# Forming the down-projection's weight sums in the stage that uses them, in an encoder block on one core

## The chip, the cores and the metric

The kernel runs on one core of one Trainium2 chip. The time is the device time of one execution in microseconds; 3 runs of the kernel before gave a median of 3151.03 us, from 3148.64 to 3153.19 us. A core has TensorE for matmuls, VectorE, ScalarE and GpSimd for elementwise work, each with its own instruction order, and here the queue of SyncE, from which the transfers between HBM and the on-chip memory are issued, one after the other. In the rows these are PE (PEld for its weight loads), DVE, ACT, POOL and SP.

## What is computed

One layer of an encoder on 2048 tokens of 1024 numbers in float32: a norm, an input projection, two groups of heads (a gated linear recurrence in both directions, and a latent attention), an output projection with residual, a second norm, a gated feed-forward part with residual, and a last norm. The change lies in the feed-forward part, whose inner width is 2816:

```python
h = _rmsnorm(x, norm2_g[l])
x = x + (jax.nn.silu(h @ w_gate[l]) * (h @ w_up[l])) @ w_down[l]
return _rmsnorm(x, final_norm_g)
```

## The kernel before

Every product is taken three times: an operand is split into a high part, rounded by ScalarE (names ending in h), and a **remainder** (ending in l), the operand less the high part, formed by VectorE or GpSimd. `mm3` (lines 193 to 195) multiplies high by high, high by remainder and remainder by high into the same bank. Splitting below means both steps.

The two large products of the feed-forward part are done as a scheme with seven products P1 to P7 in place of eight (Strassen's, in Winograd's form): both factors are cut into 2 x 2 blocks, and the seven products take blocks or sums of blocks. On the weight side these are B11 for P1, B21 for P2, B22 for P3, and the sums T4 for P4, T1 for P5, T2 for P6 and T3 for P7 (`B_OF`); T1 = B12 - B11, T3 = B22 - B12, T2 = B22 - T1, T4 = B21 - T2. The other side has A11, A12, A22, S1 to S4 (`A_OF`).

**Out-projection and second norm** (lines 1153 to 1192) go tile by tile over 16 token tiles. Each writes its part of the seven operands of the next stage to HBM (`h2_d`); `op_raw` reads them back in four pieces each, through a ring of three buffers, and `op_split` splits them with ScalarE (line 975) and VectorE (976).

**Gate and up** run in two halves (`hf`) of 1024 tokens, 22 rounds each, a round being one column block of 128 of the inner width. A round is seven products (`product`) of 12 matmuls. `r_load` loads its four weight pieces of 256 KB (B11, B12, B22, B21; line 993), all four at the time when the round before has its P1 prepared; `t_make` forms the four sums on GpSimd (line 1002), `b_make` splits, five products ahead of use (lines 1017 and 1019). `after` combines the banks on VectorE and ScalarE (lines 1079 to 1090) and stores the results g and their sums to HBM. At the end of the first half the last round's products release the operands of that half, and the seven operands of the second are loaded and split there (`late`).

**Down sums.** In the first half, `down_sums` (called 22 times, beside P2) reads four pieces of `w_down` of 128 KB (line 1061), forms the sums T1 to T4 with four operations on VectorE (1062 to 1065) and stores them in HBM (`wt_d`, line 1068). All this uses a ring of five buffers.

**Down** has 66 steps, P1, P2, P6, P7, P4, P5 with 11 steps each, of 24 matmuls into eight banks, and then P3 in eight parts of 33 matmuls. For each step `g_op` loads 512 KB of g (ring of three) and splits it on ScalarE (1253) and VectorE (1254), and `w_op` loads 256 KB of weights, a block of `w_down` or a sum from `wt_d` (ring of four, `wr`), and splits it on ScalarE (1244, names dh) and GpSimd (1245, names dl), two steps ahead. In the P5 steps `w_op` also prepares the P3 weights. When a product's last step is done, `down_after` combines its banks on VectorE, and `residual` adds x on GpSimd (line 1267): 16 times after P7, while P4 runs.

Instructions of an engine run in the order that a scheduler in the program's build has found from the program's dependences; the code above is only where they come from. A buffer of a ring is taken again when its readers are done, so a load can wait, and with it all that stands behind it on SyncE's queue.

## Time and profile before

| | before |
|---|---|
| median of 3 runs | 3151.03 us (3148.64 to 3153.19) |
| the profiled execution | 3152.19 us |
| its span, first to last instruction | 3150.4 us |
| TensorE busy | 2995.2 us, 95% of the span, 16377 matmuls |
| VectorE / ScalarE / GpSimd busy | 1915.5 (61%) / 1258.1 (40%) / 1119.5 (36%) us |
| mean granted clock of TensorE | 0.983 of full speed |
| read from HBM / written | 230.84 / 133.17 MB |

The profiled execution's own time is 1.8 us longer than its span and 1.2 us above the median. Gate and up begin at about 1780 us, the second half at about 2260, the down stage runs from about 2700 us, its P4 from 2950, its P5 from 3014, P3 from 3075. The granted clock has two levels, 1.2 and 2.4 GHz; a figure between them is a mean over the stretch. Busy time of a pipelined engine is no measure of its speed, so the number of matmuls in a stretch is read with it. A few matmul records are missing in a trace, so counts are compared with counts.

### The profile page before, as it was taken

The numbers are of one execution on the slowest core, as the hardware profiler recorded it, in microseconds if no ns is written. First come the engines' busy times: TensorE is split into PE (matmuls) and PEld (weight loads), VectorE is DVE, ScalarE is ACT, GpSimd is POOL, SyncE is SP. The second block draws the span as 40 slices with busy tenths as digits, with TensorE's granted clock in tenths as the row PEclk, the third lists the DMA queues.
The fourth block names the chain that finished last, engine by engine and source line by source line (L and its number), as shares of the span: only waits on it lengthen the run. The fifth ranks groups of instructions, "written<-read, shape, count | busy, mean of one in ns | idle before, by whom it ended". The sixth has DMA issues, their size and how long they took to land.

```text
span 3150.4 us, 45441 instructions
## 1 busy us (share of the span) xinstructions
PE 2995.2 (95%) x16377; PEld 2497.9 (79%) x16377; DVE 1915.5 (61%) x4074; ACT 1258.1 (40%) x2365; POOL 1119.5 (36%) x998
## 2 busy tenths in 40 slices
PE   7999999999789999999989888899999999999998
PEld 6899877777677888888877666788778888888786
DVE  6116557777676888888888776644654444433236
ACT  5101366666324555555533332233433333333243
POOL 1110232332332121111023554566556665234552
PEclk9999999999899999999999999999999999999999
DMA  5221112222553011100267566533433333645544
GB/s 177 72 64 55 61 60 86 80 84 80 200 189 107 28 46 34 34 24 23 94 186 226 166 210 197 187 101 101 142 119 101 104 104 97 219 154 176 183 138 153
DMA packets 335936, 366.99 MB, mean 116 GB/s; under 512 B 23480, under 2 KB 246240, under 8 KB 335712
## 3 DMA queue, kind: packets, MB, share of 16 engines
q1 hardware_dynamic: 330016, 357.00, 35.3%
q0 software_dynamic: 4608, 4.20, 0.5%
...
HBM read 230.84 MB, written 133.17 MB: 116 GB/s over the span
## 4 chain that ended last, share of the span: by engine, by line
PE 59%; DVE 8%; DMA 6%; issue 2%; POOL 1%; ACT 1%; SPq 1%; DVEq 0%; ACTq 0%; POOLq 0%
PE pd_P L195 4%; PE pd_P L194 4%; PE pd_P L193 4%; PE t L885 3%; PE pb L193 3%; PE pb L194 3%; PE pb L195 3%; PE pa L193 2%; PE pc L195 2%; PE pc L194 2%; PE pc L193 2%; PE pa L195 2%; PE pa L194 2%; PE s L852 2%; PE o L193 2%
## 5 line engine op out<-in xcount | busy, mean ns | idle before, releaser
L198 ACT ACTIVATE pth<-t 128x512 fp32r<-128x512 f32 x256 | 153.8, 603 | 249.2 <-PE t L885 249.2
L1254 DVE TENSOR_TENSOR gl_P<-gr_P,gh_P 128x1024 fp32r<-128x1024 f32 x66 | 91.1, 1381 | 218.8 <-ACT gh_P L1253 217.4
L194 PE MATMUL pd_P<-dl_P,gh_P 128*128 128x512 f32 x528 | 206.5, 391 | 3.8 <-POOL dl_P L1245 3.8
L859 DVE TENSOR_REDUCE mx<-s 128x1 f32<-128x512 f32 x256 | 175.6, 687 | 55.7 <-PE s L852 55.6
L193 PE MATMUL pd_P<-dh_P,gh_P 128*128 128x512 f32 x528 | 206.2, 391 | 0.2 <-DVE t1d L1316 0.2
L195 PE MATMUL pd_P<-dh_P,gl_P 128*128 128x512 f32 x528 | 206.1, 390 | 0.0
L868 ACT ACTIVATE pr<-s,nb 128x512 f32<-128x512 f32 x256 | 172.9, 690 | 15.2 <-DVE nb L862 11.3
L199 DVE TENSOR_TENSOR ptl<-t,pth 128x512 fp32r<-128x512 f32 x256 | 175.2, 686 | 2.5 <-ACT pth L198 0.5
L193 PE MATMUL o<-pth,vh 128*128 128x256 f32 x512 | 164.7, 322 | 0.3 <-DVE nb L862 0.3
L885 PEld LDWEIGHTS t<-ident,pr 128*128 128x128 f32 x1024 | 126.4, 140 | 40.3 <-issue 1.7
L885 PE MATMUL t<-ident,pr 128*128 128x128 f32 x1024 | 153.9, 273 | 4.1 <-DVE pr L875 2.9
L1253 ACT ACTIVATE gh_P<-gr_P 128x1024 fp32r<-128x1024 f32 x66 | 69.9, 1059 | 189.1 <-PE pd_P L194 172.0
L195 PE MATMUL o<-pth,vl 128*128 128x256 f32 x512 | 143.9, 281 | 0.0
L194 PE MATMUL o<-ptl,vh 128*128 128x256 f32 x512 | 143.9, 281 | 0.0
L651 POOL CAST qh<-qraw 128x256 fp32r<-128x256 f32 x31 | 12.4, 401 | 351.3 <-PE s L849 351.2
L875 DVE TENSOR_SCALAR pr<-pr,ri 128x512 f32<-128x512 f32 x256 | 128.3, 516 | 2.2
L194 PEld LDWEIGHTS pd_P<-dl_P,gh_P 128*128 128x128 f32 x528 | 99.4, 188 | 25.5 <-POOL dl_P L1245 4.8
L1002 POOL TENSOR_TENSOR T<-B12r,B11r 128x512 f32<-128x512 f32 x44 | 63.8, 1449 | 153.9 <-DMA B12r<-in_w_up_dram 153.9
L193 PEld LDWEIGHTS pd_P<-dh_P,gh_P 128*128 128x128 f32 x528 | 99.5, 188 | 21.6 <-DVE t1d L1316 0.6
L195 PEld LDWEIGHTS pd_P<-dh_P,gl_P 128*128 128x128 f32 x528 | 99.5, 189 | 20.7
L487 POOL TENSOR_TENSOR Am<-az 64x128 f32<-64x128 f32 x64 | 44.2, 690 | 195.3 <-DVE az L484 171.2
L1085 DVE TENSOR_TENSOR U<-t,pb 128x512 f32<-128x512 f32 x44 | 30.1, 685 | 134.0 <-PE pb L195 134.0
...
## 6 DMA issues: line engine op xcount, KB each, us to landing
s_gA<-g SPq DMA_DIRECT2D x66, 256.0 KB, 3.1
s_gS<-gS SPq DMA_DIRECT2D x66, 256.0 KB, 2.5
...
B11r<-in_w_gate_dram SPq DMA_DIRECT2D x44, 256.0 KB, 2.9
B12r<-in_w_up_dram SPq DMA_DIRECT2D x44, 256.0 KB, 2.9
B22r<-in_w_up_dram SPq DMA_DIRECT2D x44, 256.0 KB, 3.2
B21r<-in_w_gate_dram SPq DMA_DIRECT2D x44, 256.0 KB, 3.3
```

What stands on the lines that cost most here:

```text
L193: PE.matmul(ps, a_hi, b_hi, start=first, stop=False, skip_group_check=more)
L194: PE.matmul(ps, a_hi, b_lo, start=False, stop=False, skip_group_check=more)
L195: PE.matmul(ps, a_lo, b_hi, start=False, stop=last, skip_group_check=more)
L198: ACT.activation(hi, ps, AF.Copy)
L199: DVE.tensor_tensor(lo, ps, fr(hi), op=ALU.subtract)
L859: last_mx[0] = DVE.tensor_reduce(mx[:, b:b + 1], ps, op=ALU.max, axis=AX.X)
L868: ACT.activation(PR[i][:, b, :], SB[i][b], AF.Exp, scale=SCALE, bias=nb, accum_out=rs[:, b:b + 1])
L875: DVE.tensor_scalar(PR[i][:, b, :], PR[i][:, b, :], ri, None, op0=ALU.mult)
L885: PE.transpose(ps[:, j, :], PR[i][:, b, j * P:(j + 1) * P], ident)
L1002: POOL.tensor_tensor(R[nm, n], R[a, n], R[b, n], op=ALU.subtract)
L1253: ACT.activation(hi, raw, AF.Copy)
L1254: DVE.tensor_tensor(lo, raw, fr(hi), op=ALU.subtract)
```

## The change

`down_sums` and its HBM arrays go. `w_op` loads blocks of `w_down` alone and forms the sums itself on GpSimd: for P6 T3 = B22 - B12 and T2 = T3 + B11 (three loads, two operations), both kept on chip (pool `ft`); P7 takes the kept T3, without a load; P4 forms T4 = B21 - T2 from the kept T2; P5 forms T1 = B12 - B11 (two loads). The ring `wr` keeps its four buffers. The pools for the P3 weights and operands are opened only at P5's first step, after `ft` is closed.

In gate and up, `r_load` is called with names and spread over a round: B11 and B12 with P1, B22 with P6, B21 with P2; the ring has seven buffers for six, that of T four for five, that of g six for five, that of `op_raw` four for three. In the first round, A12, S1 and S3 are read through a pool of their own with five buffers, each as a group ahead of a product, and A22 and S4 are asked for earlier. At the half change an operand is split after the next product, not the one after that. The diff:

```diff
-    def op_raw(hf, i):
+    def op_raw(hf, i, pl=None, bufs=4):
...
-            raws.append(fwr.tile([P, 512], F32, tag="opraw", name=f"opr_{hf}_{i}_{j}", bufs=3))
+            raws.append((pl or fwr).tile([P, 512], F32, tag="opraw", name=f"opr_{hf}_{i}_{j}", bufs=bufs))
...
-    def r_load(n):
-
+    def r_load(n, *which):
+
+        if n >= len(seq):
+            return
         hf, f = seq[n]
         fs = slice(f * P, (f + 1) * P)
-        for nm, w_, k0 in (("B11", w_gate, 0), ("B12", w_up, 0), ("B22", w_up, 512), ("B21", w_gate, 512)):
-            raw = R[nm, n] = fwr.tile([P, 4, P], F32, tag="raw", name=f"{nm}r_{n}", bufs=6)
-            SP.dma_start(out=raw, in_=w_[0, k0:k0 + 512, fs].rearrange("(k p) f -> p k f", p=P))
+        for nm in which:
+            k0 = 0 if nm[1] == "1" else 512
+            raw = R[nm, n] = fwr.tile([P, 4, P], F32, tag="raw", name=f"{nm}r_{n}", bufs=7)
+            SP.dma_start(out=raw, in_=(w_gate if nm[2] == "1" else w_up)[0, k0:k0 + 512, fs].rearrange(
+                "(k p) f -> p k f", p=P))
...
-            if n + 1 < len(seq):
-                r_load(n + 1)
+        r_load(n + 1, *{"P1": ("B11", "B12"), "P6": ("B22",), "P2": ("B21",)}.get(pr, ()))
...
+        if late:
+            op_split(*late.pop())
         if n == NF - 1:
-            late.append([m + 2, op_raw(1, A_OF[pr])])
-        while late and late[0][0] <= m:
-            op_split(*late.pop(0)[1])
+            late.append(op_raw(1, A_OF[pr]))
...
-    def down_sums(j):
-
-        fp, c = j // 2, (j % 2) * 256
-        r = {}
-        for nm in ("B11", "B12", "B22", "B21"):
-            f, n0 = fp + (NF // 2 if nm[1] == "2" else 0), (int(nm[2]) - 1) * 512 + c
-            r[nm] = FW["dt"].tile([P, 256], F32, tag="dt", name=f"dt{nm}_{j}", bufs=5)
-            SP.dma_start(out=r[nm], in_=w_down[0, f * P:(f + 1) * P, n0:n0 + 256])
-        t1 = FW["dt"].tile([P, 256], F32, tag="dt", name=f"dtT1_{j}", bufs=5)
-        DVE.tensor_tensor(t1, r["B12"], r["B11"], op=ALU.subtract)
-        DVE.tensor_tensor(r["B12"], r["B22"], r["B12"], op=ALU.subtract)
-        DVE.tensor_tensor(r["B22"], r["B22"], t1, op=ALU.subtract)
-        DVE.tensor_tensor(r["B21"], r["B21"], r["B22"], op=ALU.subtract)
-        for nm, a in zip(TS, (t1, r["B22"], r["B12"], r["B21"])):
-            SP.dma_start(out=wt_d[nm][:, fp, c:c + 256], in_=a)
...
+        with ExitStack() as es_t:
+            first = es_t.enter_context(pool("first", side="right"))
+            op_split(*op_raw(0, "A12", first, 5))
...
+            for m in range(5):
+                if m == 0:
+                    raws[2] = op_raw(0, "S1", first, 5)
+                elif m == 2:
+                    raws[3] = op_raw(0, "S3", first, 5)
+                elif m == 3:
+                    a22 = op_raw(0, "A22")
...
-        raw = fs.tile([P, 512], F32, tag="wr", name=f"{nm}d_{fp}", bufs=4)
-        if nm in TS:
-            SP.dma_start(out=raw, in_=wt_d[nm][:, fp, :])
+
+        def wd(nm):
+            f, n0 = fp + (NP if nm[1] == "2" else 0), (int(nm[2]) - 1) * 512
+            raw = fs.tile([P, 512], F32, tag="wr", name=f"{nm}d_{pr}_{fp}", bufs=4)
+            SP.dma_start(out=raw, in_=w_down[0, f * P:(f + 1) * P, n0:n0 + 512])
+            return raw
...
+        if nm == "T2":
+            t3, raw = kept("T3"), kept("T2")
+            POOL.tensor_tensor(t3, wd("B22"), wd("B12"), op=ALU.subtract)
+            POOL.tensor_tensor(raw, t3, wd("B11"), op=ALU.add)
+        elif nm == "T3":
+            raw = KEPT["T3", fp]
+        elif nm == "T4":
+            raw = wd("B21")
+            POOL.tensor_tensor(raw, raw, KEPT["T2", fp], op=ALU.subtract)
+        elif nm == "T1":
+            raw = wd("B12")
+            POOL.tensor_tensor(raw, raw, wd("B11"), op=ALU.subtract)
```

How the order moves is shown at three places. In the rows the names carry the number of the round or step (`B12r_4` is B12 of round 4, `dl_P5_6` the remainder for step 6 of P5).

The first is SyncE's queue in gate and up, from the load of B11 for round 4 on. Before:

```order
L993 DMA B11r_4_19318<-in_w_gate_dram 128x4x128
L1068 DMA s_wtT1_16799<-dtT1_1_19566 128x256
L1068 DMA s_wtT3_16801<-dtB12_1_19560 128x256
L993 DMA B12r_4_19320<-in_w_up_dram 128x4x128
L1049 DMA s_gA11_16792<-g_1_0_19214 128x512
L1068 DMA s_wtT2_16800<-dtB22_1_19562 128x256
L1068 DMA s_wtT4_16802<-dtB21_1_19564 128x256
L1061 DMA dtB11_2_19734<-in_w_down_dram 128x256
L1049 DMA s_gA22_16797<-g_2_1_19308 128x512
L1049 DMA s_gS1_16795<-gS1_1_19365 128x512
L1049 DMA s_gS3_16796<-g_2_0_19143 128x512
L1049 DMA s_gS2_16793<-gS2_1_19366 128x512
```

And in the changed kernel:

```order
L996 DMA B11r_4_19318<-in_w_gate_dram 128x4x128
L1052 DMA s_gA11_16792<-g_1_0_19210 128x512
L996 DMA B12r_4_19320<-in_w_up_dram 128x4x128
L996 DMA B22r_4_19372<-in_w_up_dram 128x4x128
L1052 DMA s_gA22_16797<-g_2_1_19308 128x512
L1052 DMA s_gS1_16795<-gS1_1_19361 128x512
L1052 DMA s_gS3_16796<-g_2_0_19151 128x512
L1052 DMA s_gS2_16793<-gS2_1_19362 128x512
L996 DMA B21r_4_19409<-in_w_gate_dram 128x4x128
L1052 DMA s_gA12_16794<-g_1_1_19358 128x512
```

The loads and stores of the down sums (`dt`, `s_wt`) are gone from between, B22 now follows B12 at once, and the stores of g and its sums stand where they stood.

The second is GpSimd in the P6 steps, where before there is one remainder per step:

```order
L1245 TENSOR_TENSOR dl_P6_0_27020<-T2d_0_27017,dh_P6_0_27019 128x512
L1245 TENSOR_TENSOR dl_P6_1_27056<-T2d_1_27053,dh_P6_1_27055 128x512
L1245 TENSOR_TENSOR dl_P6_2_27116<-T2d_2_27113,dh_P6_2_27115 128x512
L1245 TENSOR_TENSOR dl_P6_3_27160<-T2d_3_27157,dh_P6_3_27159 128x512
L1245 TENSOR_TENSOR dl_P6_4_27196<-T2d_4_27193,dh_P6_4_27195 128x512
```

And in the changed kernel, where `T3k` and `T2k` are the kept sums:

```order
L1241 TENSOR_TENSOR T3k_3_26804<-B22d_P6_3_26806,B12d_P6_3_26808 128x512
L1242 TENSOR_TENSOR T2k_3_26805<-T3k_3_26804,B11d_P6_3_26811 128x512
L1241 TENSOR_TENSOR T3k_4_26848<-B22d_P6_4_26850,B12d_P6_4_26852 128x512
L1255 TENSOR_TENSOR dl_P6_1_26695<-T2k_1_26685,dh_P6_1_26694 128x512
L1242 TENSOR_TENSOR T2k_4_26849<-T3k_4_26848,B11d_P6_4_26855 128x512
L1241 TENSOR_TENSOR T3k_5_26892<-B22d_P6_5_26894,B12d_P6_5_26896 128x512
L1242 TENSOR_TENSOR T2k_5_26893<-T3k_5_26892,B11d_P6_5_26899 128x512
L1255 TENSOR_TENSOR dl_P6_2_26763<-T2k_2_26753,dh_P6_2_26762 128x512
L1241 TENSOR_TENSOR T3k_6_26936<-B22d_P6_6_26938,B12d_P6_6_26940 128x512
```

Between two remainders there are now two sums, which run three to four steps ahead of the remainders.

The third is GpSimd in the P5 steps, before with two remainders per step, that of P3's weight and that of P5's own:

```order
L1245 TENSOR_TENSOR dl_P3_3_28580<-B22d_3_28577,dh_P3_3_28579 128x512
L1245 TENSOR_TENSOR dl_P5_4_28532<-T1d_4_28529,dh_P5_4_28531 128x512
L1245 TENSOR_TENSOR dl_P3_4_28622<-B22d_4_28619,dh_P3_4_28621 128x512
L1245 TENSOR_TENSOR dl_P5_5_28574<-T1d_5_28571,dh_P5_5_28573 128x512
L1245 TENSOR_TENSOR dl_P3_5_28670<-B22d_5_28667,dh_P3_5_28669 128x512
L1245 TENSOR_TENSOR dl_P5_6_28616<-T1d_6_28613,dh_P5_6_28615 128x512
L1245 TENSOR_TENSOR dl_P3_6_28712<-B22d_6_28709,dh_P3_6_28711 128x512
```

And in the changed kernel, where `B12d_P5_6` becomes T1 in place:

```order
L1250 TENSOR_TENSOR B12d_P5_6_28338<-B12d_P5_6_28338,B11d_P5_6_28340 128x512
L1255 TENSOR_TENSOR dl_P3_4_28350<-B22d_P3_4_28347,dh_P3_4_28349 128x512
L1255 TENSOR_TENSOR dl_P5_5_28299<-B12d_P5_5_28293,dh_P5_5_28298 128x512
L1250 TENSOR_TENSOR B12d_P5_7_28389<-B12d_P5_7_28389,B11d_P5_7_28391 128x512
L1255 TENSOR_TENSOR dl_P3_5_28401<-B22d_P3_5_28398,dh_P3_5_28400 128x512
L1255 TENSOR_TENSOR dl_P5_6_28344<-B12d_P5_6_28338,dh_P5_6_28343 128x512
L1250 TENSOR_TENSOR B12d_P5_8_28434<-B12d_P5_8_28434,B11d_P5_8_28436 128x512
L1255 TENSOR_TENSOR dl_P3_6_28446<-B22d_P3_6_28443,dh_P3_6_28445 128x512
L1255 TENSOR_TENSOR dl_P5_7_28395<-B12d_P5_7_28389,dh_P5_7_28394 128x512
```

A sum stands ahead of each pair, two steps ahead of its own remainder; the pairs keep their order, the P3 remainder of one step and then the P5 remainder of the next.

## Rows read from the trace of the kernel before

In a timeline or a group, L1245 is the line, then come the engine, the operation and what it writes and reads; a bracket or the last column gives the idle time before it and what ended it. In the table by stretch, after the stretch and its length, stand the busy us of PE, PEld, DVE, ACT and POOL with their counts, the granted clock, the DMA engines' busy share, and GB/s.

**Rows 1.** Busy time by stretch, core 0; (x) counts instructions, PEclk granted clock.

```profile
1780.00:1840.00 60.00, 45.52 (x176) 33.60 (x176) 41.76 (x50) 27.34 (x47) 40.18 (x29) 0.91 0.66 197
1840.00:2040.00 200.00, 174.58 (x697) 138.58 (x696) 127.48 (x180) 49.99 (x83) 101.49 (x75) 0.92 0.61 194
2040.00:2240.00 200.00, 200.00 (x866) 162.55 (x866) 92.64 (x116) 62.16 (x103) 119.44 (x92) 1.00 0.33 106
2260.00:2320.00 60.00, 51.52 (x205) 41.02 (x204) 40.12 (x46) 26.50 (x46) 35.13 (x24) 0.91 0.55 167
2760.00:2880.00 120.00, 120.00 (x531) 99.38 (x530) 34.34 (x34) 42.78 (x66) 39.71 (x22) 1.00 0.45 149
3000.00:3060.00 60.00, 59.82 (x264) 49.22 (x263) 18.49 (x18) 27.52 (x48) 33.17 (x22) 1.00 0.51 163
```

**Rows 2.** Waits, 1840 to 2040: engine, line, releaser, total us, times, longest.

```profile
POOL T L1002 <- DMA B12r<-in_w_up_dram: 51.3, 9, 6.4
DVE dtT L1063 <- DMA dtB<-in_w_down_dram: 48.1, 15, 5.5
...
PE pb L193 <- DVE U L1085: 25.0, 8, 5.7
```

**Rows 3.** Timeline of SyncE's queue at 1910: start, us, what is issued, count.

```profile
1910.90 2.04 SPq L1068 DMA_DIRECT2D s_wtT<-dtB  x3
...
1913.51 0.40 SPq L993 DMA_DIRECT2D B12r<-in_w_up_dram  x1
```

**Rows 4.** Waits, 1776 to 1845.

```profile
PE pc L193 <- ACT S1h L975: 6.1, 1, 6.1
...
PE pa L193 <- ACT A12h L975: 3.8, 1, 3.8
```

**Rows 5.** Waits, 2250 to 2302.

```profile
ACT S4h L975 <- DMA opr_S<-s_h2S: 5.9, 4, 2.5
...
PE pb L193 <- ACT S4h L975: 4.5, 1, 4.5
...
PE pb L193 <- DVE U L1085: 4.0, 1, 4.0
```

**Rows 6.** GpSimd's groups, 2690 to 3070: shapes, count, busy us, mean ns, idle before.

```profile
L1245 POOL TENSOR_TENSOR dl_P<-T1d,dh_P 128x512 fp32r<-128x512 f32 x11 | 21.8, 1981 | 5.1 <-ACT dh_P L1244 5.1
L1245 POOL TENSOR_TENSOR dl_P<-T2d,dh_P 128x512 fp32r<-128x512 f32 x11 | 19.9, 1806 | 40.0 <-ACT dh_P L1244 40.0
...
L1245 POOL TENSOR_TENSOR dl_P<-B22d,dh_P 128x512 fp32r<-128x512 f32 x11 | 14.2, 1298 | 21.7 <-ACT dh_P L1244 21.6
```

**Rows 7.** DMA issues, 2690 to 3070: count, KB, median us to landing.

```profile
B11d<-in_w_down_dram SPq DMA_DIRECT2D x11, 256.0 KB, 4.9
...
B22d<-in_w_down_dram SPq DMA_DIRECT2D x11, 256.0 KB, 3.0
```

**Rows 8.** Timeline of TensorE, late in P4: start, us, matmul, idle before.

```profile
2985.26 0.50 PE L194 MATMUL pd_P<-dl_P,gh_P 128*128 128x512 f32 x1 [2.42 <-POOL dl_P L1245]
...
2986.78 0.63 PE L194 MATMUL pd_P<-dl_P,gh_P 128*128 128x512 f32 x1
...
2990.17 0.40 PE L193 MATMUL pd_P<-dh_P,gh_P 128*128 128x512 f32 x1
```

**Rows 9.** Timeline of GpSimd in P5.

```profile
3006.58 2.06 POOL L1245 TENSOR_TENSOR dl_P<-T1d,dh_P 128x512 fp32r<-128x512 f32 x1 [0.17 <-ACT dh_P L1244]
...
3013.47 2.06 POOL L1245 TENSOR_TENSOR dl_P<-T1d,dh_P 128x512 fp32r<-128x512 f32 x1 [0.17 <-ACT dh_P L1244]
...
3037.53 1.30 POOL L1245 TENSOR_TENSOR dl_P<-B22d,dh_P 128x512 fp32r<-128x512 f32 x1 [1.00 <-ACT dh_P L1244]
```

**Rows 10.** Timeline of SyncE's queue in P5.

```profile
3008.67 0.33 SPq L1242 DMA_DIRECT2D B22d<-in_w_down_dram  x1
...
3023.34 0.33 SPq L1242 DMA_DIRECT2D B22d<-in_w_down_dram  x1
...
3038.86 0.33 SPq L1242 DMA_DIRECT2D B22d<-in_w_down_dram  x1
```

More of the change, by code (lines that the diff above doesn't have):

```diff
@@ L1000, in t_make @@
             else:
-                R[nm, n] = fwr.tile([P, 4, P], F32, tag="T", name=f"{nm}_{n}", bufs=5)
+                R[nm, n] = fwr.tile([P, 4, P], F32, tag="T", name=f"{nm}_{n}", bufs=4)
             POOL.tensor_tensor(R[nm, n], R[a, n], R[b, n], op=ALU.subtract)
@@ L1176, in block_kernel @@
             if t == 13:
-                r_load(0)
+                r_load(0, "B11", "B12", "B22", "B21")
             if t == 14:
@@ L1191, in block_kernel @@
         AHEAD = 5
-        op_split(*op_raw(0, "A12"))
-        for m in range(3, AHEAD):
-            b_make(m)
-        for m in range(5):
-            nxt = slots[m + 1]
-            if nxt[1] in ("P5", "P7"):
-                op_split(*op_raw(0, A_OF[nxt[1]]))
-            product(m)
-            after(slots[m][1], slots[m][0])
-        drain(ch_n)
+        with ExitStack() as es_t:
+            first = es_t.enter_context(pool("first", side="right"))
+            op_split(*op_raw(0, "A12", first, 5))
+            raws = {}
+            for m in range(3, AHEAD):
+                b_make(m)
+            for m in range(5):
[5 more added lines that the diff above has]
+                    a22 = op_raw(0, "A22")
+                if m in raws:
+                    op_split(*raws[m])
+                product(m)
+                after(slots[m][1], slots[m][0])
+            drain(ch_n)
     fwC = es_g.enter_context(pool("fwC", side="right"))
@@ L1206, in block_kernel @@
     OPOOL.update({i: fwC for i in ("A22", "S4")})
-    FW.update({i: fw for i in ("g", "gS1", "gS2", "gS4", "dt")})
+    FW.update({i: fw for i in ("g", "gS1", "gS2", "gS4")})
     for m in range(5, len(slots)):
@@ L1211, in block_kernel @@
         if m in (5, 7):
-            op_split(*op_raw(0, A_OF[slots[m + 1][1]]))
+            op_split(*a22)
+            if m == 5:
+                a22 = op_raw(0, "S4")
         product(m)
         after(pr, n)
-        if pr == "P2" and 2 <= n < 2 + NF - 2:
-            down_sums(n - 2)
-            if n >= NF - 2:
-                down_sums(n)
     es_g.close()
@@ L1232, in tok, with kept @@
         return 8 * (i // 4) + 4 * h + i % 4
+    KEPT = {}
     def w_op(pr, fp, pl, tag, bufs):
         nm = B_OF[pr]
-        raw = fs.tile([P, 512], F32, tag="wr", name=f"{nm}d_{fp}", bufs=4)
-        if nm in TS:
-            SP.dma_start(out=raw, in_=wt_d[nm][:, fp, :])
-        else:
-            f, n0 = fp + (NP if nm[1] == "2" else 0), (int(nm[2]) - 1) * 512
-            SP.dma_start(out=raw, in_=w_down[0, f * P:(f + 1) * P, n0:n0 + 512])
+        def wd(nm):
[3 more added lines that the diff above has]
+            return raw
+        def kept(nm):
+            KEPT[nm, fp] = ft.tile([P, 512], F32, tag=f"{nm}{fp}", name=f"{nm}k_{fp}")
+            return KEPT[nm, fp]
+        if nm == "T2":
[10 more added lines that the diff above has]
+            POOL.tensor_tensor(raw, raw, wd("B11"), op=ALU.subtract)
+        else:
+            raw = wd(nm)
         hi, lo = (pl.tile([P, 512], F32R, tag=f"{tag}{c}", name=f"d{c}_{pr}_{fp}", bufs=bufs) for c in "hl")
@@ L1334, in block_kernel @@
     LW, GL = [], {}
-    fl = ctx.enter_context(pool("fl", side="right"))
+    es_k2 = ctx.enter_context(ExitStack())
+    ft = es_k2.enter_context(pool("ft", side="right"))
     def last_g(i):
@@ L1350, in block_kernel @@
         d_make(m + 2)
+        if (pr, fp) == ("P5", 0):
+            es_k2.close()
+            lw = ctx.enter_context(pool("lw", side="right"))
+            fl = ctx.enter_context(pool("fl", side="right"))
         if pr == "P5":
```

7 lines of the change are left out of this document (2 added, 5 removed).

## Prediction

> **What bounds the kernel now.** I read the page's head first (the table above): TensorE is busy 95% of the span, so time can be won only where it stands still or runs at the lower clock. Next the busy time and matmul counts by stretch [rows 1], which say where that is. An undisturbed 200 us of gate/up (2040 to 2240) has 866 matmuls, 0.231 us each as counted; the down stage has 531 in 120 us, 0.226 us each, so a step of 24 lasts 5.4 us. Against that rate three stretches are short:
>
> - 1840 to 2040: 697 matmuls instead of 866, that is 169 x 0.231 = 39.0 us lost, at a mean granted clock of 0.92;
> - 1780 to 1840, where gate/up begins: 176 instead of 260, 84 x 0.231 = 19.4 us;
> - 2260 to 2320, where the second half's operands are loaded: 205 instead of 260, 12.7 us.
>
> In the down stage 3000 to 3060, most of its P5 steps, is full but for 0.2 us. The third view is what the engines waited for in 1840 to 2040 [rows 2]: TensorE 25.0 us for line 1085 on VectorE, VectorE's line 1063 48.1 us for the down-weight pieces, GpSimd's line 1002 51.3 us for gate/up weights. The sums stand ahead of line 1085 on VectorE, and their loads and stores ahead of the weights on the one SyncE queue: three stores of sums hold it from 1910.90 for 2.04 us, and the load of B12 comes only at 1913.51 [rows 3].
>
> **Part 1, down sums out of gate/up.** 22 calls go, each with four loads, four stores and four VectorE operations. The same kind of round, without them, follows at 2040 to 2240 with TensorE 200.00 of 200 us busy [rows 1]. So up to 39.0 us come back. The new loads of a round come at three products instead of one, with 7 buffers for 6; the last of them, B21, is asked for three products ahead of its use, 3 x 12 x 0.231 = 8.3 us, where a load of that size took 3.0 to 4.9 us [rows 7]. I allow 2 us for rounds in which it comes late behind a store, and 11 us at the far end, one wait of 1 us in each of them: gain 37, bounds 28 to 39.
>
> **Part 2, operands of the first round.** TensorE waited 3.8 us for A12's split and 6.1 us for S1's [rows 4]. A12's four pieces now have five buffers and are asked for together, S1's follow at once, A22's come early; S3 and S4 still stand behind the last norm tile's stores on SyncE. I take these two waits, 10 us; bounds 4 (S1 still late) and 15 (most of the 19.4).
>
> **Part 3, the half change.** 28 pieces are split one after the other while ScalarE waits for each load (5.9 us for S4's alone), and TensorE waited 4.5 us for S4 and 4.0 us for line 1085 [rows 5]. A fourth buffer lets one more load be under way, and the split comes a product earlier. VectorE is busy 40.1 of these 60 us [rows 1] and stays so. I take half of the 12.7 us, 6.5; bounds 1 and 11.
>
> **Part 4, the sums in the down stage.** They are 44 GpSimd operations of 128x512. The nearest rows are the same engine's subtraction of that size: 1.30 us on the mean for B22's, the least, 1.81 and 1.98 us for T2's and T1's, which run beside VectorE's work on g [rows 6]. In the P6 steps GpSimd then has three operations, 3.9 to 5.9 us per 5.4 us step; in P7 no new one, in P4 and P5 one more each. They are hidden as long as they finish ahead of TensorE.
>
> *P6.* Three loads per step share a ring of four buffers. T3's operation frees two of them, a load then takes 3.0 us as B22's did [rows 7], and the next T3 follows: 3.0 + 0.2 + 1.3 to 1.98 = 4.5 to 5.2 us, or 0.5 to 1 us more where the split's remainder of an earlier step stands between. The step is 5.4 us, and GpSimd starts these sums during the last P2 steps, some three steps ahead. I take 0; the far bound is 11 x 0.9 = 10 us (a load of 4.9 us, as B11's median was earlier in the stage [rows 7]; the cycle is then 6.4 us at least, and the lead is spent in part).
>
> *P4.* Here the one existing stall sits: GpSimd adds 16 residuals between the remainders, TensorE waits 2.42 us for one at 2985.26, and the clock then falls: the matmul at 2986.78 lasts 0.63 us, and eight of them, up to 2990.17, take 3.4 instead of 1.8 us [rows 8]. Seven sums stand among these operations now. Two of them delay the late remainder beyond the load waits that are there already, 2 x 1.3 = 2.6. I take 2.5; bounds 0 and 8 (five of them, 6.5, and another clock fall of 1.6).
>
> *P5.* B12, B11 and the P3 weight B22 share the ring. In the new order SyncE's load of B22 waits for the P5 remainder of the same step, the P3 remainder for that load, and the next P5 remainder stands behind it. Exactly this loop is in the trace: the remainder from 3006.58 ends at 3008.64, B22 is issued at 3008.67, and the next T1 remainder starts at 3013.47, a cycle of 6.9 us; two more such cycles lie between the issues of 3008.67 and 3023.34, 7.3 us each. Later B22 waits for the P3 remainder only (issued 3038.86, that one ended 3038.83), and the loop is open [rows 9, 10]. So the early long cycles ate slack, no later one did, and TensorE stayed full [rows 1]. Worked along the new order with 3.0 us loads, 0.6 us splits and 1.3 to 2.06 us remainders, P5's remainder is about 4 us early at step 0, 3 at step 4, 0 at step 5, and then loses some 1.3 us (6.7 against 5.4) in each of steps 6 to 9, about 5 us. Each small idle may bring the clock fall, of which I add 2: cost 7, bounds 0 (loads land in 2.5) and 18 (7.5 us cycles from step 1 on, eight of them, 17).
>
> That beside-work price deserves a second look. A remainder that ran beside VectorE's operation took 2.06 us and one alone 1.30 [rows 6, 9], so it was delayed by 0.76 us at most. The Trainium skill (SBUF — State Buffer, section "SBUF: two separate sides") says that VectorE with two SBUF inputs and GpSimd hold a shared port pair as an exclusive lock for a whole instruction, and the loser fully blocks. By it a remainder could wait for all of VectorE's 1.4 us, the P5 cycle would be some 0.6 us longer and the sum 2 to 3 us higher; no row here shows so long a delay, so this stays out of the sum.
>
> **The sum.** -37 - 10 - 6.5 + 0 + 2.5 + 7 = -44. The profiled execution took 3152.2 us, 1.8 us outside its span, and lies 1.2 us above the median of 3151.03. 3152.2 - 44 = 3108 us.
>
> **The rivals.**
>
> *The down stage hides everything.* If loads land like the shorter ones and the start gives nearly all back: -39 - 15 - 8 = -62, 3090 us. For it: GpSimd was mostly idle there (39.7 of 120 us busy), and TensorE has not waited in 3000 to 3060 [rows 1]. Against it: the 6.9 us cycles that are in the rows already.
>
> *Gate/up stays partly stalled.* The rounds of 1840 to 2040 might be slow for the first half's loads and the clock (0.92) as much as for the sums; or the spread loads, each behind stores of g on SyncE, come late for line 1002. If half is recovered: -19 - 6 - 3 + 3 + 0 = -25, 3127 us. For it: line 1002's wait is for gate/up weights, not for the sums [rows 2]. Against it: the next 200 us have the same loads and no loss.
>
> *The ring of four decides (slower).* Loads per P6 step go from one to three and per P5 step from two to three, with no buffer more. If a sum has to wait for each load in turn, a step's cycle is load + sum + remainder, 4.9 + 1.98 + 1.98 = 8.9 us in P6 and P5 alike, and 22 steps lose (8.9 - 5.4) x 22 = 77 us: -53.5 + 77 = +23, 3176 us. It decides from 53.5 / 22 = 2.4 us per step, a cycle of 7.9 us. For it: B22's loop above already takes 6.9 to 7.3 us. Against it: the two loads of T3 are issued together, and P6 has three steps of lead.
>
> *Little moves.* The change does what it says, but part of the ring's cost (some 45 us) cancels the gain: about 3150 us.
>
> **How the numbers follow.** Chances: the forecast with its own range of 3095 to 3122 us 0.60, all hidden 0.14, half recovered 0.14, little moves 0.05, the ring decides 0.07. 0.2% is 6.3 us, about what a measurement of this kernel can tell from no change. The first three are faster by more than that, 0.88; little moves is within it, 0.05; the ring gives slower, 0.07. The range takes in most of the forecast and of its two neighbours and leaves out the last two: 3086 to 3134 us.
>
> **What would show it.** Right: 1840 to 2040 with some 860 matmuls and a clock near 1.0, no down-weight piece in gate/up; 20 us back between 1780 and 2320 outside that; in the down stage P6 full, a stall of 4 to 5 us near the eighth step of P4, and TensorE waiting for P5's remainders in the last four or five steps with B22 loads behind each. Wrong: TensorE idle in P6 on a remainder (the ring is too short), waits for B21 or B22 in every gate/up round, or no stall in P5 at all.

## The result and the profile after

The changed kernel takes 3127.72 us (median of 5 runs, 3119.84 to 3136.29), the kernel before beside it 3153.19 us (5 runs); the ratio is 0.9922, with a 95% interval of 0.9899 to 0.9945. So it is faster by some 25 us, where 44 were forecast: the time lies within the stated range of 3086 to 3134 us, well above its middle, and outside the forecast's own range of 3095 to 3122 us. The profiled execution took 3131.85 us, 4.1 above that median, so the two traces lie 20.3 us apart, and the parts below add up to that.

The page of the changed kernel, its span and two of its engines (busy us, share, instructions):

```profile
span 3130.1 us, 45080 instructions
...
PE 2985.8 (95%) x16377; PEld 2491.0 (80%) x16377; DVE 1920.2 (61%) x3986; ACT 1256.7 (40%) x2365; POOL 1210.5 (39%) x1042
```

GpSimd has the 44 more operations and is busy 91 us longer, although 44 x 1.3 is 57: its operations also became longer. TensorE has the same matmuls. The table by stretch of the changed kernel, to be read beside [rows 1] (stretch, length, busy us and counts of PE, PEld, DVE, ACT and POOL, granted clock, DMA share, GB/s):

```profile
1780.00:1840.00 60.00, 52.65 (x207) 38.92 (x206) 51.00 (x54) 28.10 (x48) 48.84 (x33) 0.94 0.67 197
1840.00:2040.00 200.00, 200.00 (x867) 162.67 (x866) 104.63 (x114) 62.10 (x103) 130.68 (x94) 1.00 0.33 104
2200.00:2260.00 60.00, 48.24 (x190) 38.40 (x189) 48.63 (x54) 28.83 (x51) 30.49 (x21) 0.89 0.58 175
2782.00:2850.00 68.00, 61.46 (x262) 49.72 (x261) 19.48 (x19) 21.97 (x38) 47.87 (x31) 0.97 0.59 188
2912.00:2978.00 66.00, 61.29 (x262) 49.78 (x262) 20.71 (x19) 15.81 (x20) 49.45 (x34) 0.97 0.56 181
2978.00:3050.00 72.00, 62.62 (x264) 49.93 (x264) 19.55 (x19) 27.32 (x48) 45.60 (x31) 0.98 0.51 159
```

The second row is the gain: 867 matmuls where 697 stood, at the full clock. The third is the half change, now near 2230, still short of 260 by 70. The last three are P6, P4 and P5: none of them is full now, where in the kernel before P6 and P5 were.

To say how much each part gave or took, I read two series of times off the timelines of both kernels: when ScalarE copies the bank of P1 in each gate/up round, and when VectorE first combines a bank at the end of each product of the down stage. Their differences, in us:

| stretch | before | after | difference | forecast |
|---|---|---|---|---|
| start to P1 of round 2 | 1837.7 | 1829.9 | -7.8 | -10 |
| rounds 2 to 11 | 214.7 | 174.9 | -39.8 | -37 |
| rounds 11 to 21 | 194.2 | 194.2 | 0 | 0 |
| half change, rounds 21 to 24 | 71.2 | 74.7 | +3.5 | -6.5 |
| rounds 24 to 43, and on to P1 of down | 449.1 | 448.7 | -0.4 | 0 |
| P2 | 58.5 | 58.5 | 0 | 0 |
| P6 | 59.8 | 68.9 | +9.1 | 0 |
| P7 | 59.9 | 59.8 | 0 | 0 |
| P4 | 64.3 | 66.8 | +2.5 | +2.5 |
| P5 | 60.3 | 72.3 | +12.0 | +7 |
| rest | 80.6 | 81.3 | +0.7 | 0 |
| span | 3150.4 | 3130.1 | -20.3 | -44 |

Up to the down stage the changed kernel is 44.5 us ahead; the down stage gives 24 of them back. The stretches of the down stage end where VectorE begins to combine, not where TensorE ends its product; this matters in some of the experiments below.

**P6.** TensorE waits there three times for a remainder, and the longest wait, 4.29 us, has this before it (timeline of GpSimd, then of TensorE, in the changed kernel: start, us, line, operation, idle before and releaser):

```profile
2814.40 1.28 POOL L1255 TENSOR_TENSOR dl_P<-T2k,dh_P 128x512 fp32r<-128x512 f32 x1
...
2819.36 1.29 POOL L1247 TENSOR_TENSOR B21d_P<-B21d_P,T2k 128x512 f32<-128x512 f32 x1
2822.56 1.92 POOL L1247 TENSOR_TENSOR B21d_P<-B21d_P,T2k 128x512 f32<-128x512 f32 x1 [1.91 <-DMA B21d_P<-in_w_down_dram]
2824.45 1.25 POOL L1255 TENSOR_TENSOR dl_P<-T2k,dh_P 128x512 fp32r<-128x512 f32 x1
...
2825.75 0.75 PE L194 MATMUL pd_P<-dl_P,gh_P 128*128 128x512 f32 x1 [4.29 <-POOL dl_P L1255]
```

Line 1247 is T4, a sum for P4, two products later. Four of these stand in GpSimd's order ahead of P6's remainders for steps 6 and 7, and the second waits for its own load. The remainder behind it, for which TensorE stands still, could have run long before: ScalarE had its high part at 2808.86, and TensorE stands from 2821.46 on. The three waits are 6.5 us together; most of the other 2.6 us of P6's loss is the lower clock, 0.97 on the mean over the product where it was 1.00 in the kernel before.

**P5.** Its first loss is at its beginning (timelines of ScalarE, VectorE and TensorE in the changed kernel):

```profile
2982.18 0.63 ACT L1254 ACTIVATE dh_P<-B22d_P 128x512 fp32r<-128x512 f32 x1 [10.52 <-DMA B22d_P<-in_w_down_dram]
...
2983.79 1.45 DVE L1264 TENSOR_TENSOR gl_P<-gr_P,gh_P 128x1024 fp32r<-128x1024 f32 x1 [6.61 <-ACT gh_P L1263]
2985.16 4.26 DVE L1326 TENSOR_TENSOR t1d<-t1d,pd_P 128x512 f32<-128x512 f32 x7
...
2985.89 0.50 PE L193 MATMUL pd_P<-dh_P,gh_P 128*128 128x512 f32 x1 [4.06 <-DVE t1d L1326]
```

ScalarE waits 10.52 us for the first B22 of P3; behind it stands the split of g, behind that its remainder on VectorE, and behind that the operations that free P4's banks, for one of which TensorE waits 4.06 us. In the kernel before, the same wait was 0.2 us. The second loss is the loop that the prediction named (GpSimd's, SyncE's and TensorE's timelines, late in P5):

```profile
3026.48 2.00 POOL L1255 TENSOR_TENSOR dl_P<-B12d_P,dh_P 128x512 fp32r<-128x512 f32 x1 [0.20 <-ACT dh_P L1254]
...
3028.51 0.33 SPq L1232 DMA_DIRECT2D B22d_P<-in_w_down_dram  x1
...
3033.41 2.03 POOL L1255 TENSOR_TENSOR dl_P<-B12d_P,dh_P 128x512 fp32r<-128x512 f32 x1 [0.17 <-ACT dh_P L1254]
...
3040.48 2.03 POOL L1255 TENSOR_TENSOR dl_P<-B12d_P,dh_P 128x512 fp32r<-128x512 f32 x1 [0.17 <-ACT dh_P L1254]
...
3035.49 0.51 PE L194 MATMUL pd_P<-dl_P,gh_P 128*128 128x512 f32 x1 [1.21 <-POOL dl_P L1255]
...
3042.57 0.50 PE L194 MATMUL pd_P<-dl_P,gh_P 128*128 128x512 f32 x1 [1.30 <-POOL dl_P L1255]
```

The remainder ends at 3028.48, B22 is issued at 3028.51, the next remainders start 6.93 and 7.07 us later, and TensorE waits 1.2 to 1.3 us in each step. The forecast was a cycle of 6.7 us and 1.3 us a step. All waits in P5 come to 9.4 us of the 12.0; the granted clock is 0.98.

### The profile page after: what moved, and what is told of

The parts are those of the page before. It is cut to its first block, busy times and chain, and to the rows that moved or that the text cites. A ratio compares the mean times of both kernels' runs of the same rounds, so it can differ in the third digit from the quotient of the medians.

```text
span 3130.1 us, 45080 instructions
## 1 busy us (share of the span) xinstructions
PE 2985.8 (95%) x16377; PEld 2491.0 (80%) x16377; DVE 1920.2 (61%) x3986; ACT 1256.7 (40%) x2365; POOL 1210.5 (39%) x1042
## 4 chain that ended last, share of the span: by engine, by line
PE 58%; DVE 6%; DMA 6%; POOL 3%; issue 2%; ACT 2%; SPq 0%; DVEq 0%; ACTq 0%; POOLq 0%
PE pb L194 4%; PE pb L193 4%; PE pb L195 4%; PE t L885 3%; PE pc L194 2%; PE pa L193 2%; PE pc L195 2%; PE pa L194 2%; PE pa L195 2%; PE pc L193 2%; PE pd_P L194 2%; PE pd_P L195 2%; PE pd_P L193 2%; PE s L852 2%; PE o L193 2%
## 5 line engine op out<-in xcount | busy, mean ns | idle before, releaser
L199 DVE TENSOR_TENSOR ptl<-t,pth 128x512 fp32r<-128x512 f32 x256 | 174.8, 684 | 2.8 <-ACT pth L198 0.5
L651 POOL CAST qh<-qraw 128x256 fp32r<-128x256 f32 x31 | 12.4, 400 | 352.7 <-PE s L849 352.6
L1073 DVE TENSOR_TENSOR t<-t,pb 128x512 f32<-128x512 f32 x44 | 30.3, 688 | 162.8 <-PE pb L195 162.8
```

Of the source, the lines that this page charges most:

```text
L199: DVE.tensor_tensor(lo, ps, fr(hi), op=ALU.subtract)
```

## The experiments

A table of all kernels, with the same stretches as above (us; single profiled executions; medians with their ratio to the kernel before where several runs were taken). The two kernels called "no sums" leave the sums out and take one block of the weights in their place:

| kernel | to round 2 | rounds 2-11 | half change | P6 | P4 | P5 | P4 + P5 | span | time, ratio [95%] |
|---|---|---|---|---|---|---|---|---|---|
| before | 1837.7 | 214.7 | 71.2 | 59.8 | 64.3 | 60.3 | 124.6 | 3150.4 | |
| changed | 1829.9 | 174.9 | 74.7 | 68.9 | 66.8 | 72.3 | 139.1 | 3130.1 | 3127.7, 0.9922 [0.9899, 0.9945] |
| no sums in before | 1836.3 | 174.7 | 72.5 | 59.8 | 66.2 | 60.0 | 126.2 | 3114.1 | 3115.6, 0.9870 [0.9849, 0.9890] |
| no sums in changed | 1827.6 | 174.9 | 71.9 | 59.8 | 65.2 | 59.9 | 125.2 | 3102.2 | 3104.8, 0.9840 [0.9813, 0.9867] |
| split later | 1829.7 | 174.9 | 70.7 | 69.2 | 66.5 | 70.4 | 136.9 | 3125.4 | 3127.2, one run |
| three operand buffers | 1833.1 | 174.8 | 70.9 | 68.3 | 67.2 | 70.8 | 138.0 | 3126.8 | 3128.5, one run |
| ring of six | 1830.2 | 174.9 | 75.4 | 68.4 | 72.7 | 65.8 | 138.5 | 3129.9 | 3131.6, 0.9932 [0.9916, 0.9949] |
| T4 on VectorE | 1828.0 | 174.9 | 71.7 | 63.7 | 63.3 | 68.2 | 131.5 | 3112.2 | 3114.0, one run |
| T4 placed | 1834.3 | 174.9 | 71.1 | 63.2 | 67.6 | 68.2 | 135.8 | 3120.5 | 3122.7, 0.9907 [0.9892, 0.9922] |
| T4 placed, ring of six | 1832.2 | 174.9 | 76.1 | 62.1 | 73.7 | 65.5 | 139.2 | 3126.5 | 3124.4, 0.9911 [0.9894, 0.9928] |
| all placed | 1836.5 | 174.9 | 76.0 | 59.8 | 68.3 | 67.2 | 135.5 | 3125.2 | 3127.0, one run |
| all placed, ring of six | 1830.1 | 174.8 | 72.3 | 59.8 | 65.1 | 66.1 | 131.2 | 3109.8 | 3112.4, 0.9869 [0.9852, 0.9885] |
| the same, T4 on VectorE | 1832.9 | 174.9 | 76.2 | 59.9 | 66.1 | 64.7 | 130.8 | 3116.7 | 3115.5, 0.9876 [0.9861, 0.9890] |
| all placed, own ring for P3 | 1829.2 | 174.9 | 75.3 | 59.8 | 68.5 | 64.9 | 133.4 | 3117.5 | 3118.9, 0.9889 [0.9866, 0.9911] |

The start and the half change are the same code in ten of these (the changed kernel and all whose edit lies in the down stage), and yet the half change takes 71.1 to 72.3 us in four of them and 74.7 to 76.2 us in six, and round 2 begins up to 9 us apart. So a span says less on the down stage than the stretch itself, and the medians of the runs may carry such shifts too.

With the ring of six, and with it and T4 placed, VectorE begins to combine P4's banks some 5 us late. P4's stretch then has 20 matmuls more and P5's 20 fewer, so some 4.6 us of P5 stand under P4 there; for these two kernels only the sum of P4 and P5 can be compared. With T4 on VectorE P4's stretch begins late instead and has 5 matmuls fewer, 1.2 us.

### What the sums cost in gate and up

```diff
-        if pr == "P2" and 2 <= n < 2 + NF - 2:
-            down_sums(n - 2)
...
+        nm = {"T1": "B12", "T2": "B22", "T3": "B22", "T4": "B21"}.get(nm, nm)
```

> The kernel before, with the down sums left out of gate and up and nothing else changed (the down stage reads a block of the down weights where it read a sum, so the work left out is the 88 loads, 88 stores and 88 VectorE operations). Theory A, the sums alone stalled the rounds: rounds 2 to 11 take 19.4 us each, the first rows of gate and up and the half change stay (three rounds of about 71 us at the half change), the down stage keeps about 60 us per product; span 3150 - 40 = 3110 us. Rival, the old grouping of the weight loads or the late first operands stalled them: no more than 15 us come back, 3135 us or more.

Rounds 2 to 11 fell from 214.7 to 174.7 us, all of the 40 us, with the weight loads still in one group and the old rings; the start (1836.3) and the half change (72.5) stayed as they were. The table by stretch of that kernel:

```profile
1840.00:2040.00 200.00, 200.00 (x866) 162.57 (x865) 100.71 (x118) 62.16 (x103) 125.95 (x93) 1.00 0.33 107
```

That is [rows 1] at 2040 to 2240, two hundred us earlier. The rival, that the grouped loads or the late first operands stalled these rounds, falls. Which part of the sums it was, their operations on VectorE, their place on SyncE's queue or their bytes, this run doesn't separate, since all three go. The spread loads of the change give nothing measurable in the steady rounds: 174.9 us with them, 174.7 without.

### What the sums cost in the down stage

```diff
-        if nm == "T2":
-            t3, raw = kept("T3"), kept("T2")
...
+        if nm[0] == "T":
+            raw = wd({"T1": "B12", "T2": "B22", "T3": "B22", "T4": "B21"}[nm])
```

> The changed kernel with the sums of the down stage left out: each step loads one block of the down weights and there are no sums on GpSimd. Theory: all that the changed kernel lost in the down stage comes from the sums and their loads, 9.1 us in P6, 2.4 in P4, 12.0 in P5; span 3130 - 23 = 3107 us, every product but P4 about 60 us long. Rival, part of it comes from the moved pools or the order: P6 or P5 still 64 us or longer.

The span is 3102.2 us, P6 59.8 and P5 59.9. By stretch:

```profile
2760.00:2880.00 120.00, 120.00 (x531) 99.42 (x530) 37.68 (x39) 40.42 (x61) 50.74 (x31) 1.00 0.50 163
2900.00:2960.00 60.00, 56.69 (x242) 46.26 (x242) 15.26 (x13) 16.33 (x21) 38.36 (x26) 0.97 0.60 196
2960.00:3025.00 65.00, 65.00 (x288) 53.62 (x287) 24.22 (x25) 29.86 (x56) 32.67 (x20) 1.00 0.42 134
```

Only the old stall in P4 is left (56.69 of 60 us). So what the down stage lost is due to the sums and their loads, 9.1 us in P6, 1.6 in P4 and 12.4 in P5, and not to the moved pools. The 1.6 us of P4 are not more than its scatter: the three kernels without sums on GpSimd have 64.3, 65.2 and 66.2 us there. How they do it, by order, by the ring or by GpSimd's time, is what the later runs tell apart.

### The half change and the start

```diff
-        if late:
-            op_split(*late.pop())
         if n == NF - 1:
-            late.append(op_raw(1, A_OF[pr]))
+            late.append([m + 2, op_raw(1, A_OF[pr])])
+        while late and late[0][0] <= m:
+            op_split(*late.pop(0)[1])
```

> The changed kernel with the split of an operand at the half change put back to two products later; four buffers stay. At the half change the changed kernel takes 74.8 us for three rounds, the kernel before 71.3, undisturbed ones 58.3. Theory A, the earlier split makes ScalarE and VectorE stand in line ahead of the banks' work: 71 us or less, 4 us won or more. Rival, the fourth buffer lets the operand loads crowd SyncE's queue: 74 to 76 us.

```diff
-    def op_raw(hf, i, pl=None, bufs=4):
+    def op_raw(hf, i, pl=None, bufs=3):
```

> The changed kernel with three buffers for the operand pieces again; the split stays one product later. Theory A (the earlier split costs): 74 to 78 us for the three rounds at the half change, since fewer loads are under way. Rival (the fourth buffer costs): 71 us.

Both gave 71 us, 70.7 and 70.9, so neither theory is borne out, and since ten executions of the changed order spread from 71.1 to 76.2 us, one run each can't tell. What holds: neither edit brings the 6.5 us that the prediction forecast; none of the fourteen profiles has a half change shorter than 70.7 us. The changed kernel's trace shows what is last there, VectorE (timelines of VectorE and TensorE):

```profile
2245.52 4.02 DVE L976 TENSOR_TENSOR S4l<-opr_S,S4h 128x512 fp32r<-128x512 f32 x3
2249.46 1.75 DVE L1022 TENSOR_TENSOR B21l<-B21r,B21h 128x512 fp32r<-128x512 f32 x1
2251.13 0.67 DVE L1069 TENSOR_TENSOR U<-t,pb 128x512 f32<-128x512 f32 x1
...
2251.95 0.77 PE L193 MATMUL pb<-A22h,T4h 128*128 128x512 f32 x1 [6.66 <-DVE U L1069]
```

TensorE waits 6.66 us for the combination of a bank, which stands behind four remainders. These take 0.7 us alone and up to 1.75 us here. VectorE is busy 48.63 of 60 us, and without a gap from 2232.17 to the end of that combination; a fourth buffer for the loads can't help there, as far as this trace shows.

The start differs between the two: P1 of round 0 to P1 of round 2 took 53.0 us before and 53.2 with three operand buffers, but 47.7 to 50.0 us in all with four. So 3 to 5 us of these two rounds hang on the fourth buffer, as far as one execution shows. The rest of the 7.8 us lies ahead of P1 of round 0, which comes at 1779 to 1787 us in the ten executions and at 1784.7 before, so it is not more than scatter.

### A longer ring

```diff
-            raw = fs.tile([P, 512], F32, tag="wr", name=f"{nm}d_{pr}_{fp}", bufs=4)
+            raw = fs.tile([P, 512], F32, tag="wr", name=f"{nm}d_{pr}_{fp}", bufs=6)
```

> The changed kernel with six buffers instead of four in the ring of down-weight loads, in every step. In the changed kernel P6 took 68.9 us, P4 66.8, P5 72.3; without the sums 59.8, 65.2 and 59.9. Theory A, the loads that wait for a buffer of the ring pace P5: P5 falls to 60 to 63 us. For P6 two theories: if the ring paces it, 60 to 62 us; if it is the sums of P4, which the scheduler places ahead of P6's late remainders on GpSimd, P6 stays at 66 us or more, since with six buffers six of them, not four, stand there. Span 3118 to 3122 us, or 3108 if the ring is all.

P6 stayed at 68.4 us, as the second of its theories had it, and the time is no better (3131.6 us). P5's stretch fell to 65.8 us and P4's rose to 72.7, but most of that is where the stretch ends (P4 and P5 by stretch, in the changed kernel and then in this one):

```profile
2909.80:2976.50 66.70, 61.99 (x266) 50.36 (x265) 22.23 (x20) 16.43 (x22) 51.21 (x35) 0.97 0.54 177
2976.50:3048.80 72.30, 62.92 (x265) 50.23 (x264) 19.07 (x18) 26.87 (x47) 45.60 (x31) 0.98 0.53 165
...
2910.40:2983.10 72.70, 67.56 (x285) 53.89 (x284) 21.93 (x19) 17.55 (x24) 53.02 (x38) 0.98 0.57 182
2983.10:3049.00 65.90, 58.78 (x245) 47.89 (x245) 19.18 (x20) 26.17 (x45) 38.37 (x27) 0.92 0.47 152
```

Together they took 138.5 us, 139.1 in the changed kernel. In P5 TensorE's waits for the weights (4.1 us for remainders, 1.2 for a high part) are gone, as the loop through the ring would have it; in their place its waits for P4's banks rose from 4.1 to 7.1 us, and the granted clock is 0.92 there. With more buffers the scheduler draws more of the later work ahead: six sums of P4, not four, stand ahead of P6's remainders, and P5's sums and P3's weights ahead of P4's.

### The place of P4's sums

```diff
-            POOL.tensor_tensor(raw, raw, KEPT["T2", fp], op=ALU.subtract)
+            DVE.tensor_tensor(raw, raw, KEPT["T2", fp], op=ALU.subtract)
```

> The changed kernel with the 11 sums of P4 formed on VectorE, not on GpSimd. Theory, P6 loses by the sums of P4 that stand ahead of its remainders on GpSimd: P6 62 us or less (in place of 68.9), P4 shorter by 2 or so, P5 unchanged at 70 to 72 us. Rival, GpSimd's own three operations per P6 step or the ring pace it: P6 stays at 67 us or more.

```diff
+            with tc.issue_after(LO[0].ins):
+                POOL.tensor_tensor(raw, raw, KEPT["T2", fp], op=ALU.subtract)
...
+        LO[0] = POOL.tensor_tensor(lo, raw, fr(hi), op=ALU.subtract)
```

> The changed kernel with one edge in the order: a sum of P4 is placed on GpSimd behind the remainder of the step before it, so none stands ahead of a P6 remainder; work, buffers and loads are the same. Theory, the place of P4's sums is what P6 lost by: P6 61 us or less, P4 67 to 70 us (its first sums come later), P5 as it was, span 3122 us. Rival (ring or GpSimd's share in P6): P6 67 us or more.

With the sums on VectorE P6 is 63.7 us; with the same sums left on GpSimd but behind the remainder of the step before it is 63.2 us. The work is the same in the second; only the order on one engine differs. So the place of P4's sums explains 5.7 of P6's 9.1 us, less than was expected (61 us or less). TensorE still waits in P6 of that kernel:

```profile
PE pd_P L194 <- POOL dl_P L1256: 2.8, 2, 1.7
```

P5 came down by 4 us in both, to 68.2, since the wait for P4's banks at its beginning was gone (0.2 and 0.5 us instead of 4.1).

The placement of P4's sums and the ring of six, both as in the diffs above:

> Both: six buffers in the ring, and P4's sums behind the remainder of the step before. Theory, these two are all that the down stage lost: P6 60 us, P5 60 to 63 us, P4 66 to 69 us, span 3106 to 3112 us, faster than the changed kernel by 0.6% and than the kernel before by 1.3%. If the sums still cost GpSimd's time itself, P6 or P5 stays above 65 us.

Both edits together: P6 62.1, but P4 and P5 together 139.2 us, against 135.8 with the placement alone, so this theory fell. In P5 TensorE waits for nothing but P4's banks, 6.8 us in all and 6 of them at once (VectorE's and TensorE's timelines of this kernel):

```profile
2987.53 4.26 DVE L1327 TENSOR_TENSOR t1d<-t1d,pd_P 128x512 f32<-128x512 f32 x7
...
2988.27 0.80 PE L193 MATMUL pd_P<-dh_P,gh_P 128*128 128x512 f32 x1 [5.98 <-DVE t1d L1327]
```

With six buffers P3's weights are still drawn ahead, and the chain from ScalarE's wait for B22 to P4's banks is as in the changed kernel.

### All sums and remainders in the program's order

```diff
+        with tc.issue_after(LO[0].ins):
+            return w_op1(*a)
```

Here every sum and remainder of a weight stands behind the remainder prepared before it.

> The changed kernel with every sum and remainder of a down weight placed on GpSimd behind the remainder of the step that the program prepares before it, so nothing of a later step stands ahead of an earlier one; buffers, loads and work as in the changed kernel. Theory, order for P6 and ring for P5: P6 60 to 62 us (68.9 in the changed kernel, 63.2 with only P4's sums placed), P5 still 66 us or more (72.3), because a load of B11 waits for the remainder two steps ahead of it in the ring of four, and load, sum, split and remainder in turn take 3.0 + 1.3 + 0.6 + 2.0 = 6.9 us per 5.4 us step. Rival, P5 lost by order alone: 62 us or less.

P6 is 59.8 us, all that it was without sums, though it has the same 22 sums on GpSimd and the same ring of four:

```profile
2780.00:2850.00 70.00, 70.00 (x311) 57.97 (x310) 20.89 (x22) 26.15 (x42) 50.52 (x36) 1.00 0.70 225
```

GpSimd is busy 50.52 of 70 us there and TensorE has no gap. So P6's loss is shown to be order, not GpSimd's time and not the ring. P5 is 67.2 us, 5 less than in the changed kernel and 7 more than without sums, as expected of the ring: order alone doesn't mend it.

This placement, and `bufs=6` in the ring:

> The same placement with six buffers in the ring. Theory: both causes are gone, P6 60 to 62 us, P5 60 to 62 us, P4 65 to 68 us (16 residuals and 11 sums on GpSimd), span 3106 to 3110 us. Where six buffers alone gave P4 72.7 and P5 65.8 us, because P5's sums and the P3 weights were drawn ahead of P4's remainders, this placement takes that away; if P4 stays at 72 us or P5 at 65, the order was not the reason.

The shortest of the medians with the sums: 3112.4 us, a ratio of 0.9869 to the kernel before, whose interval lies below that of the changed kernel (0.9852 to 0.9885 against 0.9899 to 0.9945). TensorE doesn't wait for P4's banks any more, 7.1 us with the ring of six alone, so the placement does take away what that ring cost. P5 is still 66.1 us, against the expectation. TensorE's waits there are 2.5 us, and the granted clock is 0.95, which is some 3 us more. Both waits stand behind one of ScalarE's (its timeline, then TensorE's):

```profile
3011.36 0.63 ACT L1261 ACTIVATE dh_P<-B22d_P 128x512 fp32r<-128x512 f32 x1 [3.87 <-DMA B22d_P<-in_w_down_dram]
...
3013.51 0.50 PE L193 MATMUL pd_P<-dh_P,gh_P 128*128 128x512 f32 x1 [1.10 <-ACT dh_P L1261]
...
3015.37 0.80 PE L194 MATMUL pd_P<-dl_P,gh_P 128*128 128x512 f32 x1 [1.36 <-POOL dl_P L1262]
```

B22 for P3, which nobody needs for 20 us, is split ahead of P5's own block on ScalarE, whose order was left to the scheduler, and its load is late.

The same once more, with T4 formed by `DVE.tensor_tensor`:

> As the one before, and P4's 11 sums on VectorE. Theory: P4's loss is GpSimd's share, 16 residuals, 11 remainders and 11 sums of 1.3 to 2.3 us in 60 us; without the sums P4 is 63 to 65 us as in the kernel before (64.3) or better (63.3 with only this move), P6 and P5 as in the one before, span 3103 to 3107 us.

P4 was 66.1 us, not 63 to 65, so the sums' share of GpSimd was not what was left in P4 here. TensorE's one wait in P4 is 4.2 us, for a remainder that stands behind residuals on GpSimd; VectorE, which now has the sums, stands 7.5 us for a load of B21, with three remainders of g behind it. The span is longer than that of the kernel with the placement and the ring of six, by 3.9 us at the half change and 2.8 at the start.

Last, the placement with four buffers in the ring, and two of their own for the P3 weights:

```diff
-            raw = fs.tile([P, 512], F32, tag="wr", name=f"{nm}d_{pr}_{fp}", bufs=4)
+            raw = fs.tile([P, 512], F32, tag="w3" if pr == "P3" else "wr", name=f"{nm}d_{pr}_{fp}",
+                          bufs=2 if pr == "P3" else 4)
```

> The placement of all sums and remainders as before, the ring of the blocks back at four buffers, and the P3 weights' loads in a ring of two of their own; the bytes are those of the ring of six. With the ring of six P5 still took 66.1 us, since ScalarE stood up to 4.3 us in wait for a load of B22 with the split of P5's own sum behind it. Theory, the P3 load that waits for a buffer which the sums hold is what remains in P5: P5 60 to 63 us, P6 59.8 us, P4 65 to 68 us, span 3104 to 3109 us. Rival, the loop of load, sum, split and remainder in a ring of four paces P5 anyway: 66 us or more, as with the placement and four buffers alone (67.2).

P5 is 64.9 us: below the rival's bound, above the theory's, so it is not decided. Of the 7.3 us that P5 loses with the placement alone, the two buffers take away 1 to 2.3, whichever way they are given. Of the remaining 5 us TensorE's waits make 4.0, 2.7 for remainders and 1.3 for high parts. What makes these late stays open; ScalarE's order in P5, which no run here changed, is the likeliest place, but that is only argued. P4's own last stall (3.2 to 4.2 us in the placed kernels, 2.4 before, 3.3 without sums) stands behind the residuals in GpSimd's order; no run moved these.

## Why the prediction was right, and where it was not

The main mechanism was right, and the time lies in the stated range. But the range was made wide for the rivals, and 3127.72 us is the figure of a rival whose mechanism was wrong: gate and up came back in full, and the down stage lost two and a half times the 9.5 us of the sum. That the time still fell inside is in part luck. One of the prediction's own signs of being wrong came true, TensorE idle in P6 on a remainder, though not because the ring was short. Another sign, 20 us back between 1780 and 2320 outside the rounds, was more than the 16.5 us of the prediction's own sum, and 4.3 came.

**Gate and up.** The largest term was right in place and size: 37 forecast, 39.8 measured, and the run without the sums alone gives 40.0. That the sums stalled these rounds is shown by that run; that they did it from both VectorE's and SyncE's order [rows 2, 3] fits it, but the two were not separated. The 2 us that I took off for the spread loads were not needed: the rounds are 19.4 us each from round 3 on.

**The start.** 10 forecast, 7.8 measured in the profile, of which 5 lie in the first two rounds and the rest is not more than scatter. The waits named, of 6.1 us for S1's high part and 3.8 for A12's [rows 4], are indeed gone from the changed kernel; in their place TensorE waits 3.7 us for the remainder of B11 on GpSimd, which was not foreseen. They are gone with three operand buffers too, and there the two rounds are as long as before (53.2 us), so taking these two waits for the gain was not borne out.

**The half change.** Here the step failed: "half of the 12.7 us" was chosen as if the loads were the last wait. The changed kernel loses 3.5 us more in the profile, and 0 to 5 more over the ten executions of this order. I had read that TensorE waited 4.5 us for S4 and 4.0 us for line 1085 [rows 5], and that VectorE was busy 40.1 of 60 us [rows 1], and yet costed only the first. The second, VectorE's combination of a bank behind its share of the splits, is what ends last now, with 11.8 us in all. VectorE was two thirds busy on the mean in the kernel before and did not stay so: it is busy 48.63 of 60 us now, and has no gap in the 20 us ahead of the longer wait.

**P6.** The term was 0 with a bound of 10, and it was 9.1. The reckoning of the ring was right: 59.8 us with four buffers and the sums in the program's order. What the step left out is the order a few rows further on. I looked at what stands between the remainders of the first steps, saw T2 and T3 of later steps of the same product, and took it that this goes on. The four sums of P4 that stand ahead of steps 6 and 7 are as plain in the order, and one of them waits for its load. Placing these sums alone gives 5.7 us back; the rest goes when the sums of later P6 steps are placed too.

**P4.** 2.5 forecast and 2.5 measured; the stall of 2.4 us [rows 8] has become two, 2.5 and 2.2 us, both on a remainder behind residuals and sums. Against the kernels without sums on GpSimd the loss is 0.6 to 2.5 us, so the agreement of the two figures may be luck.

**P5.** 7 forecast, 12.0 measured. The loop was right to the step and nearly to the tenth: TensorE waits in the last steps, 1.2 to 1.6 us each, with a cycle of 6.93 and 7.07 us where 6.7 was worked out and 6.9 had been seen [rows 9, 10]. What was left out is the other end of the same wait. ScalarE's 10.52 us for the first B22 of P3 hold up the split of g, VectorE behind it, and with it the freeing of P4's banks, 4.1 us. I asked who waits for the load on GpSimd, but not what is queued behind it on ScalarE.

**The price beside other work.** I took 0.76 us as the most that VectorE's work delays GpSimd's, and wrote that no row shows more. That was a misreading: the kernel before has longer ones, and the changed kernel too (VectorE and GpSimd in the kernel before, then in the changed one):

```profile
2826.05 1.22 DVE L1254 TENSOR_TENSOR gl_P<-gr_P,gh_P 128x1024 fp32r<-128x1024 f32 x1
2826.20 2.23 POOL L1245 TENSOR_TENSOR dl_P<-T2d,dh_P 128x512 fp32r<-128x512 f32 x1 [3.64 <-ACT dh_P L1244]
...
2802.94 1.23 DVE L1264 TENSOR_TENSOR gl_P<-gr_P,gh_P 128x1024 fp32r<-128x1024 f32 x1 [4.21 <-ACT gh_P L1263]
2802.95 2.37 POOL L1242 TENSOR_TENSOR T2k<-T3k,B11d_P 128x512 f32<-128x512 f32 x1
```

Against 1.29 us alone these are delays of 0.94 and 1.08 us. The Trainium skill (SBUF — State Buffer, section "SBUF: two separate sides") has the loser block for the other's whole instruction. That is an estimate of up to 1.23 us for these rows, the length of VectorE's remainder, and they are nearer to it than to my bound. By it P5 would have come out at 9 to 10 by the prediction's own estimate, nearer to the 12 measured, though the wait for the banks and not this price makes most of the difference.

**The rivals.** "The ring decides" named the right places, but not the size: a step took 6.3 us on the mean in P6 and 6.6 in P5, not the 7.9 us at which it would have cost the whole gain, and in P6 the loss was the order's. "The down stage hides everything" is excluded, by 24 us. "Gate/up stays partly stalled" came out nearest in time, 3127 us, for a reason that the runs refute: gate and up recovered all of it.
